# Sorting a mixture-of-experts kernel's experts by token count, and giving the 14 smallest 64 places and two products in place of three

## The chip, the cores and the metric

The kernel runs on one core of one Trainium2 chip. The time is the device time of one execution in microseconds (us). The engines are called as the profile calls them: PE (matrix products; PEld is its loading of the stationary operand), DVE (vector), ACT (scalar), POOL (general, here gathers and scatters), and SP (it issues the transfers of weights; its queue is SPq).

## The reference, cut to what matters

Two layers on 1024 tokens of width 1024. Each is a mixer (a gated convolution in layer 0, sliding-window attention in layer 1), a norm, a mixture of experts and a norm. The experts' part, with the bookkeeping left out:

```python
def hierarchical_moe(x, w_grp, w_exp, wg, wu, wd):
    ...
    g_idx = jnp.argmax(g_logits, axis=-1)          # one of 4 groups for each token
    ...
    top_p, top_i = lax.top_k(e_prob, TOP_K)        # 2 of the 8 experts of the group
    ...
    counts = jnp.zeros((N_EXPERTS,), jnp.int32).at[eid].add(1)
    ...
    def run_block(args):                           # a block: up to 128 tokens of one expert
        xb, e = args
        hid = jax.nn.silu(xb @ wg[e]) * (xb @ wu[e])
        return hid @ wd[e]
```

There are 32 experts in a layer. `wg[e]` and `wu[e]` are 1024 by 512, `wd[e]` is 512 by 1024, all float32: 6.29 MB an expert. 2048 pairs of token and expert are spread over the 32 experts as the tokens choose, so an expert has 64 on the mean, some have many more and some fewer.

## The kernel before

Every expert has a block of 128 places. An expert with more than 128 tokens gets further blocks after all the others (the overflow, `NOV`). A float32 product is made from parts: each operand is split into a high and a low part, and `mm3` (L203 to L206) makes three products, high by high, high by low, low by high. The rows of tokens are the stationary operand (128 by 128), the weights the moving one (128 by 512).

The weights come in chunks of 1 MB, six to an expert: two for gate, two for up, two for down. SP issues their transfers in the order of use, as soon as there is room in one of the rings of raw buffers (12 buffers in the first six rounds of a layer, then 6). A chunk is split by ACT, which writes the high part as a cast (L164), and by DVE, which writes the low part as a difference (L165). The parts have room for four chunks, so that the cast of chunk k waits until PE has done with chunk k-4. `split_until` issues the splits in the program's order, three chunks ahead of the products (`ahead = 3`).

`experts` (L718) is one written-out sequence, and each engine executes its own instructions in this order. For expert e, with c its first chunk, one pass of the loop at L818 issues: the products of gate with chunk c; y_out (L764, ACT scales the finished rows of expert e-2, and POOL adds them to memory, L713); the split of c+3; gate with c+1; the split of c+4; silu (L833, ACT); up with c+2; the split of c+5; the transposes of the next expert's rows (`xpose`, L735, PE) and the gather for expert e+3 (L703, POOL); up with c+3; the product of silu and up (L848, DVE); the split of c+6; the split of the next expert's rows (`xsplit`: `xh` on ACT, `xl` on DVE); the down products of expert e-1, with the splits of c+7 and c+8; and `hid_pose`, which transposes the hidden rows (L771, PE) and splits them (`hh` on ACT, `hl` on DVE). The next pass begins with the products of the next gate. So the down products of an expert stand one pass behind, and `hid_pose` stands last on PE before the next expert's first product.

Beside the first experts DVE, POOL and PE still work out the gates of the places (`gates` L600 on, `slot_gates` L630 to L641): POOL makes one-hot tables (`goh`, `ga`), and PE sums them into `pgate`.

Of the kernel before, what the change touches and what calls it, by code (L numbers as in the profile page):

```python
# [11 lines left out]
F32 = mybir.dt.float32  # L12
# [21 lines left out]

@with_exitstack
def moe_net_kernel(ctx, tc, a, dbg=None):
# [35 lines left out]
    def expert_chunks(l):  # L72
        seq = []
        for e in range(NE + 1):
            if e < NE:
                for w in ("w_gate", "w_up"):
                    for h in range(2):
                        seq.append(rows(a[w][l, e], h * 512, 512))
            if e > 0:
                for h in range(2):  # L80
                    seq.append(rows(a["w_down"][l, e - 1], h * 256, 256))
# [15 lines left out]
    # The raw chunks lie in rings of two: two rings always, except that heads of q take the second during  # L97
    # the attention, a third from the output projection to the experts' last, and four chunks in the room of
    # the mixer's output, from when it has been read to the experts' last.
    rings = []  # L100
    turn = itertools.cycle(("raw", "raw", "rawc", "rawc"))
    for l, c0 in enumerate((mark["wout"], mark["wo"])):
# [7 lines left out]
        while len(rings) < c0 + 4 + 6 * NE:  # L110
            rings += four() + ["rawb"] * 2
    raws, hs, ls = {}, {}, {}
# [4 lines left out]
    def pump(eng=nc.sync):  # L117
        while st["load"] < min(len(chunks), st["limit"]):
# [12 lines left out]
            src = chunks[i][0]  # L131
            if i == 1:
                # the first two chunks come in alternate quarters, that the work may start
# [12 lines left out]
    # 32 KB in two halves: the mixers' output, chunks, the norm's rows, heads of q  # L146
# [49 lines left out]
    def warm(n, ps, tag, bufs):  # L196
        # products for nothing where the tensor engine waits, that its clock stays up
# [12 lines left out]
    # -------------------------------------------------------------- constants  # L210
# [4 lines left out]
    diff = const.tile([P, P], F32, name="diff")  # L215
# [10 lines left out]
    iota(wt, [[-1, NE]], base=NE)  # L226
    rowm = const.tile([P, NB], F32, name="rowm")
# [37 lines left out]
    # ------------------------------------------------- bias rows of attention  # L265
# [3 lines left out]
    def bias_rows(w, ps):  # L269
# [11 lines left out]
        # row q lies q further right, so that a plain rectangle of it holds the relative positions  # L281
# [25 lines left out]
            # v, tokens on partitions  # L307
# [26 lines left out]
            # u, channels on partitions  # L334
# [1116 lines left out]
```

## Time and profile before

| | us |
|---|---|
| runs of the kernel before | 2083.45, 2084.56, 2085.84 |
| median | 2084.56 |
| span of the profiled execution | 2086.2 |
| PE busy in it | 1931.8 (93%) |
| DVE busy | 1580.8 (76%) |
| ACT busy | 1206.1 (58%) |
| POOL busy | 476.9 (23%) |

The profile gives the profiled execution no other time than its span. A busy PE means that products were under way; the granted clock (PEclk) is that of PE, as a share of full speed. Idle time of an engine counts only where another engine waits for what it does next.

### The profile page before, as it was taken

What the parts mean: (1) busy time and instruction counts of PE and PEld (TensorE: products, weight loads), DVE (VectorE), ACT (ScalarE), POOL (GpSimd) and SP (SyncE); (2) the same over time, 40 slices, a digit from 0 to 9 for tenths busy, and PEclk for the clock granted to TensorE, in tenths of its full rate; (3) what the DMA queues carried; (4) which work ended last, traced back from release to release, by engine and by line L of the source; (5) the groups of instructions that cost most, each with busy time, mean ns of one, the idle gap of its engine ahead of it and who ended that gap; (6) DMA issues with size and microseconds to landing.
All of it is one profiled execution on the core that took longest, in us unless ns stands there. A gap on an engine that the chain in (4) does not pass through costs nothing. (4 is left out here: it accounts for less than half of the span.)

```text
span 2086.2 us, 24852 instructions
## 1 busy us (share of the span) xinstructions
PE 1931.8 (93%) x9264; PEld 1565.7 (75%) x9264; DVE 1580.8 (76%) x2020; ACT 1206.1 (58%) x1246; POOL 476.9 (23%) x319
## 2 busy tenths in 40 slices
PE   8999998899999999998598989979999999999990
PEld 7888786687778888887487767757877888888870
DVE  3533587599888888887643996976898888888876
ACT  4211211477677777776454872125777777777763
POOL 0100003622111211212300552146121112112116
PEclk9999998899999999999799999989999999999995
DMA  6141536599969999997511006366999699999983
GB/s 249 41 122 41 192 112 242 192 335 371 345 228 363 371 364 377 369 371 281 225 41 62 21 21 232 125 248 219 374 357 355 218 379 360 368 376 364 380 282 145
DMA packets 97215, 527.59 MB, mean 253 GB/s; under 512 B 19668, under 2 KB 21732, under 8 KB 43840
## 3 DMA queue, kind: packets, MB, share of 16 engines
q1 hardware_dynamic: 76992, 487.41, 61.6%
q0 software_dynamic: 20096, 38.52, 7.4%
q8 instruction: 75, 1.23, 0.2%
q14 instruction: 52, 0.43, 0.1%
HBM read 501.58 MB, written 62.94 MB: 271 GB/s over the span
## 5 line engine op out<-in xcount | busy, mean ns | idle before, releaser
L165 DVE TENSOR_TENSOR l<-raw,h 128x2048 fp32r<-128x2048 f32 (+2 forms) x356 | 797.4, 2261 | 108.3 <-ACT h L164 104.0
L164 ACT CAST h<-raw 128x2048 fp32r<-128x2048 f32 (+1 forms) x363 | 678.2, 1884 | 130.9 <-PE pu L206 38.0
L713 POOL DMA_INDIRECT acc<-y,idx x64 | 127.5, 1993 | 605.7 <-ACT y L764 578.9
L204 PE MATMUL pu<-h,xh 128*128 128x512 f32 x512 | 209.5, 409 | 0.0
L204 PE MATMUL pg<-h,xh 128*128 128x512 f32 x512 | 208.6, 407 | 0.0
L204 PE MATMUL pd<-h,hh 128*128 128x512 f32 x512 | 203.2, 397 | 1.4 <-ACT hh L164 1.4
L206 PE MATMUL pg<-h,xl 128*128 128x512 f32 x512 | 203.0, 397 | 1.0 <-DVE xl L165 1.0
L206 PE MATMUL pu<-h,xl 128*128 128x512 f32 x512 | 203.1, 397 | 0.0
L205 PE MATMUL pu<-l,xh 128*128 128x512 f32 x512 | 202.9, 396 | 0.0
L206 PE MATMUL pd<-h,hl 128*128 128x512 f32 x512 | 202.0, 395 | 0.0
L205 PE MATMUL pg<-l,xh 128*128 128x512 f32 x512 | 201.7, 394 | 0.0
L205 PE MATMUL pd<-l,hh 128*128 128x512 f32 x512 | 201.4, 393 | 0.0
L703 POOL DMA_INDIRECT xg<-x1d,idx x64 | 96.6, 1510 | 354.0 <-PE pt L735 340.2
L164 ACT CAST xh<-pt 128x1024 fp32r<-128x1024 f32 x66 | 67.0, 1016 | 126.5 <-PE pu L205 110.2
L848 DVE TENSOR_TENSOR sg<-sg,pu 128x512 f32<-128x512 f32 x64 | 44.0, 687 | 110.8 <-PE pu L206 110.8
L206 PEld LDWEIGHTS pg<-h,xl 128*128 128x128 f32 x512 | 96.0, 188 | 25.2 <-DVE xl L165 1.9
L206 PEld LDWEIGHTS pd<-h,hl 128*128 128x128 f32 x512 | 96.0, 187 | 24.9 <-DVE hl L165 0.9
L206 PEld LDWEIGHTS pu<-h,xl 128*128 128x128 f32 x512 | 96.6, 189 | 23.7
L165 DVE TENSOR_TENSOR l<-ry,h 128x2048 fp32r<-128x2048 f32 x48 | 109.9, 2296 | 5.9 <-ACT h L164 5.9
L204 PEld LDWEIGHTS pd<-h,hh 128*128 128x128 f32 x512 | 96.0, 187 | 24.4 <-ACT hh L164 1.7
L205 PEld LDWEIGHTS pd<-l,hh 128*128 128x128 f32 x512 | 96.0, 187 | 23.1
L204 PEld LDWEIGHTS pu<-h,xh 128*128 128x128 f32 x512 | 97.6, 191 | 20.1
(326 smaller groups left out, 3844.8 us busy)
## 6 DMA issues: line engine op xcount, KB each, us to landing
raw<-in_w_gate SPq DMA_DIRECT2D x128, 1024.0 KB, 8.3
raw<-in_w_up SPq DMA_DIRECT2D x104, 1024.0 KB, 10.5
raw<-in_w_down SPq DMA_DIRECT2D x104, 1024.0 KB, 10.6
ry<-in_w_up SPq DMA_DIRECT2D x24, 1024.0 KB, 8.1
ry<-in_w_down SPq DMA_DIRECT2D x24, 1024.0 KB, 10.0
raw<-in_w_in SPq DMA_DIRECT2D x8, 1024.0 KB, 6.4
x1d<-xr SPq DMA_DIRECT2D x16, 512.0 KB, 2.7
acc<-xr SPq DMA_DIRECT2D x16, 512.0 KB, 3.9
```

Source lines behind the costliest of these rows:

```text
L164: (high or nc.scalar.copy)(h, x)
L165: (eng or nc.vector).tensor_tensor(l, x, h.bitcast(F32), op=OP.subtract)
L204: nc.tensor.matmul(out, sh, mh, start=start, stop=False)
L205: nc.tensor.matmul(out, sh, ml, start=False, stop=False)
L206: nc.tensor.matmul(out, sl, mh, start=False, stop=stop)
L703: nc.gpsimd.indirect_dma_start(out=rows, out_offset=None, in_=src, in_offset=bass.IndirectOffsetOnAxis(ap=idx, axis=0), bounds_check=T - 1 ...
L713: nc.gpsimd.indirect_dma_start(out=acc, out_offset=bass.IndirectOffsetOnAxis(ap=idx, axis=0), in_=rows, in_offset=None, bounds_check=T - 1 ...
L848: nc.vector.tensor_tensor(sg, sg, pu, op=OP.mult)
```

## The change

Each layer's experts are sorted on the chip by their token counts. Of the 32, the first three stay as they are (the experts 0 to 2, since their weights are loaded before the counts are known). The other 29 are put in order: 15 heavy ones, and the 14 smallest, the light ones, with 64 places each. The light ones are taken in pairs; a pair is one unit, with one gather, one set of transposes and one split for its 2 x 64 rows. The units go in the order heavy, heavy, heavy, then seven times (light pair, heavy, heavy), then a heavy one: 25 units, 32 experts.

For a light expert the high parts of its 64 rows and the low parts of the same 64 rows stand side by side as one stationary operand of 128 columns. Two products with a weight tile then make in the upper and the lower half of the result what three made, and one product that was not made before (low by low). The halves are added later: ACT copies the lower half out of `pg`, DVE adds it to the upper half, silu follows, and the same for `pu`. In the down products the hidden rows stand as [high, low, high], so that [high, low] and [low, high] serve as the two stationary operands in the three products of `mm3`; their number stays.

`sort` and `sort_gates` are new. They make ranks out of comparisons of the counts, a selection matrix from the ranks, and the order and the places by products with it. For every place from the fourth on, SP reads the expert's number from `order` and computes the address of each of the six chunks before it issues the transfer. Some scratch tiles are shared that were apart before.

```diff
+NS, NH, NL = 3, 15, 14
+CAP = 64
+UNITS = ["heavy"] * NS + ["light", "heavy", "heavy"] * (NL // 2)
+UNITS += ["heavy"] * (NS + NH + NL // 2 - len(UNITS))
...
+    def source(s):
...
+        l, p, w, r0, n = s
+        if p < NS:
+            return rows(a[w][l, p], r0, n)
+        if (l, p) not in experts_of:
+            col = PLACES[p][2]
+            experts_of[l, p] = nc.values_load(order_of[l][0:1, col:col + 1], engines=[mybir.EngineType.SP], min_val=0,
...
+        return a[w][l][bass.ds(experts_of[l, p], 1), r0:r0 + n].rearrange("o (p k) f -> p (o k) f", p=P)
...
+    def sort(w, ps, R):
...
+        nc.tensor.matmul(t[:, 0:NE], ones16, last, start=True, stop=True)
+        nc.tensor.matmul(t[e, 32:33], last, ones16[:, 0:1], start=True, stop=True)
...
+        nc.vector.scalar_tensor_tensor(key, R["cnt"][e], 64.0, orderr[e], op0=OP.mult, op1=OP.add)
+        nc.vector.scalar_tensor_tensor(own, t[e, 32:33], 64.0, orderc[e], op0=OP.mult, op1=OP.add)
+        nc.vector.tensor_scalar(more, key, own, None, op0=OP.is_gt)
+        nc.vector.tensor_reduce(place, more, axis=AX.X, op=OP.add)
...
+        nc.vector.tensor_scalar(sel[e], slots[e, 0:NE], place, None, op0=OP.is_equal)
...
+        yield
+        nc.tensor.matmul(t[0:1, 64:96], ecol[e], sel[e], start=True, stop=True)
+        nc.tensor.transpose(t[e, 128:256], ix[:, 0:NE], ident)
...
+        nc.tensor.matmul(t[:, 512:512 + NE], ixT[e], sel[e], start=True, stop=True)
...
+                    if lo is None:
+                        sh = h[:, 4 * half + k, j]
+                        nc.tensor.matmul(out, sh, hs[c][:, sl], start=first, stop=False)
+                        nc.tensor.matmul(out, sh, ls[c][:, sl], start=False, stop=last)
+                    else:
+                        mm3(out, h[:, 4 * half + k], lo[:, 4 * half + k], hs[c][:, sl], ls[c][:, sl], first, last)
...
+                    if light(p):
+
+                        nc.scalar.copy(sg[CAP:], pg[CAP:])
+                    else:
+                        nc.scalar.activation(sg, pg, AF.Silu)
...
+                    if light(p):
+                        nc.vector.tensor_tensor(sg[0:CAP], pg[0:CAP], sg[CAP:], op=OP.add)
...
-                    nc.vector.tensor_tensor(sg, sg, pu, op=OP.mult)
                     split_until(min(c + 3 + ahead, last - 1))
...
+                    if light(p):
+                        nc.scalar.activation(sg[0:CAP], sg[0:CAP], AF.Silu)
+                    else:
+                        nc.vector.tensor_tensor(sg, sg, pu, op=OP.mult)
...
+                    if p < NE - 1:
+                        split_until(c + ahead)
+                if light(p):
+                    nc.scalar.copy(sg[CAP:], pu[CAP:])
+                    nc.vector.tensor_tensor(pu[0:CAP], pu[0:CAP], sg[CAP:], op=OP.add)
+                    nc.vector.tensor_tensor(sg[0:CAP], sg[0:CAP], pu[0:CAP], op=OP.mult)
...
```

In layer 0, place 19 is the first expert of a light pair after the change. In the rows that follow, a number behind a tile's name is its chunk (133 to 135 are split with gate and the first half of up, 136 with the second half, 137 and 138 with the down products). DVE's order for this place before, from the first split of the pass to the last:

```order
682 L165 TENSOR_TENSOR l133_5588<-raw133_5447,h133_5587 128x2048
683 L165 TENSOR_TENSOR l134_5606<-raw134_5465,h134_5605 128x2048
684 L165 TENSOR_TENSOR l135_5626<-raw135_5485,h135_5625 128x2048
685 L848 TENSOR_TENSOR sg19_5611<-sg19_5611,pu19_5569 128x512
686 L165 TENSOR_TENSOR l136_5657<-raw136_5516,h136_5656 128x2048
687 L165 TENSOR_TENSOR xl20_5663<-pt20_5631,xh20_5662 128x1024
688 L165 TENSOR_TENSOR l137_5680<-raw137_5539,h137_5679 128x2048
689 L165 TENSOR_TENSOR l138_5698<-raw138_5557,h138_5697 128x2048
```

And after the change:

```order
720 L205 TENSOR_TENSOR l133_5497<-raw133_5359,h133_5496 128x2048
721 L205 TENSOR_TENSOR l134_5511<-raw134_5377,h134_5510 128x2048
722 L205 TENSOR_TENSOR l135_5527<-raw135_5397,h135_5526 128x2048
723 L1003 TENSOR_TENSOR sg19_5516<-pg19_5481,sg19_5516 64x512
724 L205 TENSOR_TENSOR l136_5542<-raw136_5427,h136_5541 128x2048
725 L205 TENSOR_TENSOR l137_5565<-raw137_5453,h137_5564 128x2048
726 L1039 TENSOR_TENSOR pu19_5482<-pu19_5482,sg19_5516 64x512
727 L1040 TENSOR_TENSOR sg19_5516<-sg19_5516,pu19_5482 64x512
728 L205 TENSOR_TENSOR l138_5586<-raw138_5471,h138_5585 128x2048
729 L925 TENSOR_TENSOR hid19_5596<-ph19_5591,hid19_5596 128x4x64
```

`sg19` by `pu19`, which stood behind three differences, is now the last of three small operations (L1003, L1039, L1040), and stands behind five differences. The split of the next rows (`xl20`) has gone from this place; it stands with the second expert of the pair.

ACT's order for the same place before:

```order
270 L164 CAST h133_5587<-raw133_5447 128x2048
271 L164 CAST h134_5605<-raw134_5465 128x2048
272 L833 ACTIVATE sg19_5611<-pg19_5568 128x512
273 L164 CAST h135_5625<-raw135_5485 128x2048
274 L164 CAST h136_5656<-raw136_5516 128x2048
275 L164 CAST xh20_5662<-pt20_5631 128x1024
276 L164 CAST h137_5679<-raw137_5539 128x2048
277 L164 CAST h138_5697<-raw138_5557 128x2048
```

And after the change:

```order
282 L204 CAST h133_5496<-raw133_5359 128x2048
283 L204 CAST h134_5510<-raw134_5377 128x2048
284 L996 COPY sg19_5516<-pg19_5481 64x512
285 L204 CAST h135_5526<-raw135_5397 128x2048
286 L204 CAST h136_5541<-raw136_5427 128x2048
287 L1018 ACTIVATE sg19_5516<-sg19_5516 64x512
288 L204 CAST h137_5564<-raw137_5453 128x2048
289 L1038 COPY sg19_5516<-pu19_5482 64x512
290 L204 CAST h138_5585<-raw138_5471 128x2048
291 L924 CAST hid19_5596<-ph19_5591 128x4x2x64
```

Silu (L833 before, L1018 after) has moved from behind two casts to behind four, and waits there for DVE's addition (L1003). Two copies from the accumulators (L996, L1038) are new, and the second stands behind the fifth cast.

## Rows read from the trace of the kernel before

**Rows 1.** The page's head.

```profile
span 2086.2 us, 24852 instructions
```

**Rows 2.** Stretch of one expert: length; busy PE, PEld, DVE, ACT, POOL; PEclk; DMA share, GB/s.

```profile
687.20:705.40 18.20, 18.20 (x86) 14.91 (x85) 15.77 (x10) 14.22 (x10) 3.59 (x2) 1.00 1.00 363
```

**Rows 3.** Waits of the DMA-issuing engine, 1890 to 1985: total, times, longest.

```profile
SPq L139 <- DVE l L165: 83.2, 31, 4.3
```

**Rows 4.** Timeline of DVE: start, duration, line, operation, tiles, count; in brackets idle before.

```profile
703.94 4.48 DVE L165 TENSOR_TENSOR l<-raw,h 128x2048 fp32r<-128x2048 f32 x2
...
709.49 6.90 DVE L165 TENSOR_TENSOR l<-raw,h 128x2048 fp32r<-128x2048 f32 x3 [0.47 <-ACT h L164]
718.21 0.69 DVE L848 TENSOR_TENSOR sg<-sg,pu 128x512 f32<-128x512 f32 x1 [1.82 <-PE pu L206]
...
721.02 1.22 DVE L165 TENSOR_TENSOR xl<-pt,xh 128x1024 fp32r<-128x1024 f32 x1
```

**Rows 5.** Timeline of PE in the same stretch.

```profile
705.40 0.63 PE L771 MATMUL ph<-ident,sg 128*128 128x128 f32 x4
705.78 0.48 PE L204 MATMUL pg<-h,xh 128*128 128x512 f32 x1
706.10 0.40 PE L205 MATMUL pg<-l,xh 128*128 128x512 f32 x1
...
707.27 0.39 PE L204 MATMUL pg<-h,xh 128*128 128x512 f32 x1
...
714.26 1.11 PE L735 MATMUL pt<-ident,xg 128*128 128x128 f32 x8
715.13 0.48 PE L204 MATMUL pu<-h,xh 128*128 128x512 f32 x1
```

**Rows 6.** Timeline of ACT in the same stretch.

```profile
706.06 0.59 ACT L164 CAST hh<-ph 128x512 fp32r<-128x512 f32 x1 [1.36 <-PE ph L771]
...
707.55 3.71 ACT L164 CAST h<-raw 128x2048 fp32r<-128x2048 f32 x2
711.67 0.60 ACT L833 ACTIVATE sg<-pg 128x512 f32<-128x512 f32 x1 [0.41 <-PE pg L206]
...
717.98 1.01 ACT L164 CAST xh<-pt 128x1024 fp32r<-128x1024 f32 x1 [1.61 <-PE pu L205]
```

**Rows 7.** Stretches with gaps of PE, and those behind them; columns of group 2.

```profile
404.00:406.60 2.60, 0.02 (x1) 0.00 (x0) 2.37 (x2) 1.82 (x1) 2.60 (x3) 1.00 0.99 413
406.60:413.40 6.80, 5.62 (x21) 4.88 (x22) 0.19 (x1) 0.00 (x0) 4.07 (x9) 0.50 0.70 271
519.10:521.00 1.90, 0.04 (x1) 0.05 (x1) 1.90 (x5) 1.90 (x2) 0.00 (x0) 1.00 1.04 379
522.60:526.10 3.50, 3.50 (x13) 2.87 (x12) 3.50 (x7) 0.60 (x1) 0.00 (x0) 0.51 1.04 332
1033.10:1036.10 3.00, 0.00 (x0) 0.00 (x0) 3.00 (x2) 0.58 (x1) 0.81 (x1) 1.00 0.05 21
1036.10:1040.00 3.90, 3.89 (x17) 3.25 (x18) 3.56 (x3) 0.00 (x0) 0.00 (x0) 1.00 0.70 248
```

**Rows 8.** Timeline of DVE where layer 0 starts its experts.

```profile
372.03 0.19 DVE L604 TENSOR_TENSOR ge<-lg,mx 128x32 f32<-128x32 f32 x1
```

**Rows 9.** Timeline of POOL in the same place.

```profile
382.78 0.37 POOL L637 TENSOR_SCALAR ga<-A,gate 128x32 f32<-128x32 f32 x1 [2.33 <-DVE gate L623]
```

**Rows 10.** Waits of PE where layer 0 starts its experts, 365 to 425.

```profile
PE pgate L630 <- POOL ga L637: 3.8, 5, 2.6
```

**Rows 11.** Waits of ACT, 1890 to 1985: total, times, longest.

```profile
ACT h L164 <- DMA raw<-in_w_gate: 7.0, 7, 1.8
```

**Rows 12.** Stretches with few transfers, and one with many; columns of group 2.

```profile
600.00:617.00 17.00, 16.43 (x79) 13.32 (x78) 15.24 (x18) 11.53 (x10) 1.55 (x2) 1.00 0.17 40
1620.00:1640.00 20.00, 19.43 (x94) 15.82 (x93) 17.78 (x19) 14.25 (x10) 3.06 (x2) 1.00 0.34 108
1003.00:1009.00 6.00, 3.22 (x14) 2.85 (x15) 5.32 (x6) 5.58 (x12) 2.31 (x3) 0.50 1.03 421
```

More of the change, by code (lines that the diff above doesn't have):

```diff
@@ L32, with places @@
 EARLY = (1, 6)
+NS, NH, NL = 3, 15, 14
+CAP = 64
+UNITS = ["heavy"] * NS + ["light", "heavy", "heavy"] * (NL // 2)
+UNITS += ["heavy"] * (NS + NH + NL // 2 - len(UNITS))
+def places():
+    out, heavy, light = [], 0, NH
+    for u, kind in enumerate(UNITS):
+        if u < NS:
+            out.append((u, 0, NH + NL + u))
+        elif kind == "heavy":
+            out.append((u, 0, heavy))
+            heavy += 1
+        else:
+            out += [(u, 0, light), (u, 1, light + 1)]
+            light += 2
+    return out
+PLACES = places()
 @with_exitstack
@@ new lines, in gather @@
+            def gather(u):
+                if u < NS:
+                    idx = R["idx"][:, u:u + 1]
+                elif u == U:
+                    idx = R["ovidx"][:, 0:1]
+                else:
+                    col = next(q[2] for q in PLACES if q[0] == u)
+                    idx = R["sidx"][:, col:col + 1]
+                    if UNITS[u] == "light":
+                        idx = R["twos"][:, (col - NH) // 2:(col - NH) // 2 + 1]
+                gather_rows(xg[(u + U) % 2], x1d, idx)
@@ new lines, in light, with gu @@
+            def light(p):
+                return p < NE and UNITS[PLACES[p][0]] == "light"
+            def gu(p, half, c, out):
+                u, j = PLACES[p][:2] if p < NE else (U, 0)
+                h, lo = xT[u]
+                for k in range(4):
+                    first, last = half == 0 and k == 0, half == 1 and k == 3
+                    sl = slice(k * 512, (k + 1) * 512)
+                    if lo is None:
+                        sh = h[:, 4 * half + k, j]
+                        nc.tensor.matmul(out, sh, hs[c][:, sl], start=first, stop=False)
+                        nc.tensor.matmul(out, sh, ls[c][:, sl], start=False, stop=last)
+                    else:
+                        mm3(out, h[:, 4 * half + k], lo[:, 4 * half + k], hs[c][:, sl], ls[c][:, sl], first, last)
@@ L753, in down @@
+            def down(p, half, c):
                 if half == 0:
-                    pd[e] = ps.tile([P, D], F32, name=f"pd{e}", tag="pd" if e < NE - 1 else "pt", bufs=1)
-                h, lo = hT[e]
+                    pd[p] = ps.tile([P, D], F32, name=f"pd{p}", tag="pd" if p < NE - 1 else "pt", bufs=1)
+                h, lo = hT[p]
                 for k in range(2):
@@ L777, in extra @@
+                hT[p] = (h, lo)
             def extra(e):
@@ L802, in experts @@
             ov = {}
-            why = "it follows from the counts"
             gather(0)
@@ L840, in experts @@
+                    gu(p, 0, c + 2, pu)
+                    next(sorting, None)
+                    split_until(min(c + 2 + ahead, last))
+                    if light(p):
+                        nc.vector.tensor_tensor(sg[0:CAP], pg[0:CAP], sg[CAP:], op=OP.add)
+                    extra(p)
+                    if ends and u + 1 < U:
+                        xpose(u + 1)
+                        if p == 0:
                             xsplit(1)
-                    if e + 3 < NE:
-                        gather(e + 3)
@@ L852, in experts @@
+                    if 0 < p < NE - 1 and ends:
+                        xsplit(u + 1)
                     c += 4
-                if e == NE:
-                    y_out(e - 2)
+                if p == NE:
+                    y_out(p - 2)
                     xe = nc.values_load(R["meta"][0:1, 1:2], engines=[mybir.EngineType.SP], min_val=0,
@@ L929, in overflow_blocks @@
             ps = pool(f"ops{l}", space=PSUM, st=s)
-            why = "it follows from the counts"
             s.enter_context(tc.If(nblk > 1))
```

237 lines of the change are left out of this document (156 added, 81 removed).

## The prediction

> **What bounds the kernel now.** I read the page's head first, then the stretches of single experts, then the timelines of PE, DVE and ACT over one of them, and last the places where PE stood still. The head gives a span of 2086.2 us [rows 1], with PE busy for 93% of it by the table above. In the middle of layer 0 one expert takes 18.20 us, and in it PE is busy for 18.20 us, DVE for 15.77 and ACT for 14.22; the 16 transfer engines have a share of 1.00 at 363 GB/s [rows 2]. So two things are full at once, PE and the transfers, and DVE follows with 87%. The share of the transfers is no proof that they limit, since SP issues one only when a raw buffer is free: late in layer 1 it stands for 83.2 us of 95 at waits for DVE's differences, which free the buffers [rows 3]. Within an expert the limit is PE, and DVE waits for it: the product of silu and up (L848) had idled 1.82 us for up [rows 4]. The reader is to see there also that DVE's other wait, 0.47 us before the first difference of a pass, is for ACT.
>
> **What is taken from PE.** Five products take 707.27 - 706.10 = 1.17 us, 0.234 each [rows 5]. A heavy expert has 48 of gate and up and 24 of down: 72 x 0.234 = 16.8 us, with 0.87 us of transposes of rows (714.26 to 715.13) and 0.38 of hidden rows (705.40 to 705.78), 18.1 us. A light expert saves 16 products, 3.74 us. For 14 in each of two layers that is 28 x 3.74 = 105 us of PE's time, about 5% of the run. Half of the pairs' transposes goes too (14 x 0.87 = 12 us). The question is whether what stands beside PE can follow.
>
> **The chain of a light expert.** I walk the new order with durations of before; t = 0 is the expert's first gate product, 705.78 in the trace.
>
> - The first difference of a pass begins at 709.49, t = 3.71 [rows 4]. What it waits for is ACT's queue: the cast of the hidden rows (706.06), y_out, and the first weight cast (707.55) [rows 6]. All three remain in the same order, and the hidden rows' cast starts from the transposes, which are the last work of the previous expert on PE. So this delay stays.
> - Three differences take 6.90 us [rows 4]: t = 10.6. ACT keeps ahead: its first two casts end at 711.26 (t = 5.5), the new copy is priced as silu, 0.60 us [rows 6], and the third cast (1.86, half of 3.71) ends by t = 8.1.
> - DVE adds the half of `pg`. This operation is not in the trace; it has the width of the product at L848, 512 elements for each partition, so 0.69 us [rows 4] is my price; half would be a lower bound, since half of the partitions is used, and a whole difference (2.24) the upper. t = 11.3.
> - Silu can only start now on ACT: t = 12.0. Behind it stands the cast of c+7, to 13.9. DVE meanwhile takes the fourth difference, to 13.6, waits 0.4 us for that cast, and takes the fifth, t = 14.0 to 16.3.
> - Only then come the addition for `pu` and the product with silu, 2 x 0.69: t = 17.7. The copy they need ran on ACT from 13.9 to 14.5.
> - The transposes of hidden rows wait for it, t = 17.75 to 18.1. That is the next expert's t = 0.
>
> PE's own work ends early: 32 products of gate and up and 24 of down take 13.1 us; it waits 0.4 us for the first difference (t = 6.0, when its 24 products are done at 5.6) and 0.4 for the second (8.3, when up is done at 7.9), and is through at t = 14.0. Then it stands still for 3.7 us. So the first expert of a pair takes 18.1 us, as a heavy one does.
>
> The second has the split of the next unit's rows as well: ACT 1.01 us [rows 6], DVE 1.22 less an overlap of 0.1 [rows 4]. Its product comes at t = 18.7, the period is 19.1, the gap 4.7. A pair takes 37.2 us for 36.4 before. With the pitch that operations have back to back (4.48 for two differences, 3.71 for two casts) it is 36.2. I take +0.4 a pair, for 14 pairs **+6 us**, with bounds of -3 and +11. The freed time of PE becomes idle time, since before, L848 stood behind three differences and waited for PE; now PE waits for it behind five.
>
> **The clock.** PE now stands still twice in a pair, for 3.7 and 4.7 us. The trace has three gaps of the kind [rows 7]. After 2.60 us of standing (404.0 to 406.6) the granted clock was 0.50, its lower level of 1.2 GHz, for 6.80 us; after 1.90 (519.1 to 521.0) it was 0.51 over 522.6 to 526.1, 3.5 us; after 3.00 (1033.1 to 1036.1) it stayed at 1.00. So gaps of this length mostly cost the clock, not always. At half clock H us of PE do the work of H/2. Where a heavy expert follows, PE is the bound and loses H/2: 1.75 us (H = 3.5) or 3.4 (H = 6.8). Where the second light follows, its gap covers it but for waits at the two half-chunks, 0.1 to 1.6 us. That makes 1.85 to 5.0 a pair. I take 2.9, nearer to the shorter fall, and that four gaps in five bring it: 2.3 x 14 = **+32 us**. Bounds: 0, and 14 x 5 = 70.
>
> **Start of each layer.** `sort` puts nine or so small DVE operations and nine products of PE ahead of the gates. A small operation of DVE takes 0.19 us here [rows 8], so they are 2 us; the products are taken as 0.234 each, 2 us. POOL's first gate table waited 2.33 us for DVE's gates [rows 9], and PE's longest wait there, 2.6 us, the gap before 406.6, is for these tables [rows 7, 10]: what delays DVE here delays PE. A result of PE reaches ACT in 0.28 us (705.78 to 706.06) [rows 5, 6], and the sort goes to and fro some six times, 1.7 us. Rounded down for what lies beside other work I take 5 us a layer, **+10 us**. Lower bound 2 (all beside PE's first experts), upper 20 (the tables' wait of 2.6 comes for each step of the sort too).
>
> **SP's reading of the order.** Its loads of registers and address arithmetic are not in the trace of before. SP waits 83.2 us of 95, for some five experts, about 16 us each [rows 3]: that is the cover, and I cost it at nothing. They count only if an expert's take longer than those 16 us, or if a chunk's landing is late already. The gathers go from 32 to 25 a layer, on POOL, which is busy for 3.59 us of 18.20 [rows 2]: nothing.
>
> **End of layer 1.** There ACT waited 7.0 us in seven waits for gate weights to land [rows 11]; slower pairs give the transfers time. **-2 us**, bounds -5 and 0.
>
> **The sum.** 6 + 32 + 10 - 2 = +46. It is made against the profiled span of 2086.2, which lies 1.6 above the median of the runs, with no other time shown for that execution; from the median 2084.6 + 46 = **2131 us**. The changes and their sizes are small beside the span, so I carry the sum over as it is.
>
> **Rivals.**
>
> *The light chain is shorter than walked (faster).* The chain is one loop: hidden transposes, ACT's three operations, five differences, product. If it runs below about 17.4 us (the additions at 0.35 because of 64 partitions, no wait for the cast of c+7, waits before the first difference shorter because PE is done early), a pair takes 35 us or less, and the gaps shrink. Then the transfers decide. They stood idle for 0.83 x 17 = 14 us at the ring's change in layer 0 and 0.66 x 20 = 13 in layer 1 [rows 12]. If 363 GB/s is what they can do, only these 27 us are to be had, less the 10 of the start: 2068. But over 1003 to 1009 they moved 421 GB/s [rows 12], 6.29 MB in 14.9 us; then pairs of 34 us would give 14 x 2.4 = 34 on top of 27 less 10, and about 2035. Against it: two of the three terms of the loop, ACT's head and the differences, are rows as they stand.
>
> The Trainium skill, "DMA: Bandwidth & Descriptors", section "Where 436 GB/s comes from", says that for transfers between memory and SBUF the memory's share of a core, about 358 GB/s, binds. By that an expert's 6.29 MB would need 17.6 us, and 64 experts could gain at most 38 us by any relief of PE, my estimate from that page. This trace disagrees: 363 is passed by the 421 of [rows 12]. So I do not use that limit.
>
> *The clock stays up (a small loss).* One gap of 3.00 us did not lower it [rows 7]. If none does, 6 + 10 - 2 = 14 remains: 2099, with the bounds of the rest 2079 to 2115.
>
> *Each gap costs the long fall (a larger loss).* With 6.8 us at half clock after each, 14 x 5.0 = 70 in place of 32: 2169; with the upper bounds of the rest, 2184.
>
> **How the numbers follow.** The forecast has a chance of 0.50 and is the likeliest, the long fall 0.12, the clock that stays 0.18, the faster chain 0.18, and 0.02 is left for cases that I have not named. Two executions of this kernel differ by about 0.1%, so 0.2% (4 us) is what can be told from no change. Faster: 0.18 and a little of the second rival, 0.20. Same: 0.06, from the second rival near its lower bound. Slower: 0.74. The forecast's own range is 2105 to 2160. The range for 8 in 10 reaches down past the lower end of the clock's rival and into the faster one, 2078, and up to 2180; the deeper gains (0.15) and the last 0.04 are left out.
>
> **What would show it.** Right: in light experts PE idles 3 to 5 us before the hidden transposes, released by DVE's product with silu, and DVE no longer waits for PE's up there; a pair of light experts takes 37 to 40 us; granted clock of 0.5 after such gaps, in the stage where it was 1.00; a transfer share below 1; PE's busy products fewer by 28 x 16. Wrong: light experts of 16 us or less; a first difference well before t = 3.7; gaps below 2 us. SP released last by its own register loads, or ACT waiting for weights that have not landed in the middle of a layer, would show that the part that I cost at nothing is not.

## The result and the profile after

| | us |
|---|---|
| runs after the change | 2119.71, 2122.60, 2123.80, 2125.53 |
| median | 2123.2 |
| median before, same chip | 2085.2 |
| ratio of the two | 1.0173, 95% interval 1.0161 to 1.0186 |
| span of the profiled execution | 2122.2 |

The medians lie 38 us apart, and the ratio makes it 36 us, 34 to 39 by its interval: slower. The page of the changed kernel, with its span, the busy times, the granted clock and the share of the transfers in 40 slices:

```profile
span 2122.2 us, 24672 instructions
...
PE 1862.6 (88%) x8728; PEld 1501.3 (71%) x8728; DVE 1613.4 (76%) x2108; ACT 1224.2 (58%) x1288; POOL 445.9 (21%) x307
...
PEclk9999998899999899899799999988999999999995
DMA  6131436599969999997511006365999699999974
```

PE is busy for 69 us less than before and the span is 36 us longer [rows 1]. PE's instructions, products and transposes, went from 9264 to 8728: 28 x 16 products and 14 x 8 transposes fewer, and a few more for the sort. Three digits of the clock's row in the expert stages went from 9 to 8 (places 14, 17 and 28).

Next two groups of light, light, heavy, heavy in layer 0, a stretch from one expert's hidden transposes to the next's; columns as in [rows 2]:

```profile
680.40:698.30 17.90, 14.05 (x62) 10.69 (x60) 16.14 (x11) 14.42 (x11) 1.59 (x1) 0.97 1.02 381
698.30:718.30 20.00, 17.07 (x69) 13.70 (x69) 17.09 (x12) 15.43 (x12) 4.35 (x2) 0.84 1.01 384
718.30:739.10 20.80, 20.80 (x84) 17.02 (x85) 15.65 (x10) 14.26 (x10) 3.15 (x2) 0.85 0.93 332
739.10:757.10 18.00, 18.00 (x86) 14.99 (x86) 15.96 (x10) 14.18 (x10) 3.15 (x2) 1.00 0.96 349
757.10:775.00 17.90, 14.07 (x62) 10.70 (x60) 16.15 (x11) 14.42 (x11) 1.58 (x1) 1.00 1.00 372
775.00:794.10 19.10, 16.23 (x68) 13.04 (x68) 17.02 (x12) 15.42 (x12) 4.34 (x2) 0.91 1.00 366
794.10:812.30 18.20, 18.16 (x84) 15.16 (x85) 15.62 (x10) 14.18 (x10) 3.22 (x2) 1.00 0.97 360
812.30:830.20 17.90, 17.90 (x85) 14.95 (x84) 15.86 (x10) 14.18 (x10) 3.15 (x2) 1.00 1.00 377
```

The first expert of a pair takes 17.9 us, not less than a heavy one, and PE is busy for 14.1 of it. The second takes 19.1 or 20.0, the heavy behind it 18.2 or 20.8, and a heavy one with nothing before it 18.0, where it was 18.2 [rows 2]. So the first group takes 76.7 us and the second 73.1, for 72.9 before. The columns of the clock tell the two apart. The gaps of the first group, and what follows each:

```profile
694.50:698.30 3.80, 0.13 (x2) 0.06 (x1) 3.73 (x4) 2.36 (x2) 0.00 (x0) 0.85 1.01 425
698.30:704.00 5.70, 5.70 (x16) 4.52 (x17) 3.92 (x3) 4.99 (x4) 1.57 (x1) 0.50 1.02 427
715.30:718.30 3.00, 0.07 (x2) 0.06 (x1) 2.94 (x4) 1.59 (x1) 0.00 (x0) 0.89 1.05 425
718.30:724.50 6.20, 6.20 (x17) 4.92 (x18) 4.43 (x3) 3.44 (x4) 1.46 (x1) 0.50 0.98 359
```

After 3.8 us of standing the clock is 0.50 for 5.7 us, and after the second gap of 3.0 us for 6.2. The two gaps of the second group, with what follows the first of them:

```profile
771.30:774.90 3.60, 0.00 (x0) 0.00 (x0) 3.54 (x4) 2.26 (x2) 0.00 (x0) 1.00 1.00 419
774.90:779.10 4.20, 4.13 (x13) 3.32 (x14) 2.47 (x3) 3.44 (x4) 1.56 (x1) 0.59 1.02 419
791.30:794.10 2.80, 0.00 (x0) 0.00 (x0) 2.73 (x4) 1.47 (x1) 0.00 (x0) 1.00 1.01 419
```

The first gap was followed by a fall again (0.59 over 4.2 us). The second left the clock at 1.00, as the stretch from 794.10 above shows, and the heavy expert behind it took 18.2 us. By the idle time that the trace gives ahead of the hidden transposes, the second gaps of the two groups are equally long: 2.93 and 2.92 us.

The DVE timeline in the first light expert, whose first gate product stands at about 680.8:

```profile
684.48 6.70 DVE L205 TENSOR_TENSOR l<-raw,h 128x2048 fp32r<-128x2048 f32 x3 [1.46 <-ACT h L204]
691.21 0.68 DVE L1003 TENSOR_TENSOR sg<-pg,sg 64x512 f32<-64x512 f32 x1
691.92 2.29 DVE L205 TENSOR_TENSOR l<-raw,h 128x2048 fp32r<-128x2048 f32 x1
694.39 2.29 DVE L205 TENSOR_TENSOR l<-raw,h 128x2048 fp32r<-128x2048 f32 x1 [0.17 <-ACT h L204]
696.72 0.69 DVE L1039 TENSOR_TENSOR pu<-pu,sg 64x512 f32<-64x512 f32 x1
697.44 0.68 DVE L1040 TENSOR_TENSOR sg<-sg,pu 64x512 f32<-64x512 f32 x1
```

The first difference begins at t = 3.7, the addition for gate ends at 11.1, the fifth difference runs from 13.6 to 15.9, and the product with silu (L1040) ends at 17.3. It is the order shown in the section on the change, with no idle time but 0.17 us. PE in the same place:

```profile
694.20 0.40 PE L246 MATMUL pd<-h,hid 128*128 128x512 f32 x1
698.27 0.71 PE L918 MATMUL ph<-ident,sg 64*128 64x64 f32 x4 [3.67 <-DVE sg L1040]
698.91 0.79 PE L886 MATMUL pg<-h,xx 128*128 128x512 f32 x1
```

The last down product starts at 694.20 and the hidden transposes 3.67 us of idle time later, released by `sg` L1040. Over the whole run the view of the tile `ph` gives for this wait, in us and times:

```profile
  DVE sg L1040: 76.6, 27
```

### The profile page after: what moved, and what is told of

It is laid out like the page before. It is cut to its first block, busy times and chain, and to the rows that moved or that the text cites. A ratio compares the mean times of both kernels' runs of the same rounds, so it can differ in the third digit from the quotient of the medians.

```text
span 2122.2 us, 24672 instructions
## 1 busy us (share of the span) xinstructions
PE 1862.6 (88%) x8728; PEld 1501.3 (71%) x8728; DVE 1613.4 (76%) x2108; ACT 1224.2 (58%) x1288; POOL 445.9 (21%) x307
## 5 line engine op out<-in xcount | busy, mean ns | idle before, releaser
L824 POOL DMA_INDIRECT acc<-y,sidx x64 | 101.4, 1585 | 721.9 <-ACT y L910 708.6
L245 PE MATMUL pd<-l,hid 128*128 128x512 f32 x512 | 201.3, 393 | 1.3 <-DVE l L205 0.6
L244 PE MATMUL pd<-h,hid 128*128 128x512 f32 x512 | 201.1, 393 | 1.4 <-ACT hid L204 1.4
L246 PE MATMUL pd<-h,hid 128*128 128x512 f32 x512 | 201.4, 393 | 0.0
L205 DVE TENSOR_TENSOR l<-ry,h 128x2048 fp32r<-128x2048 f32 x48 | 109.4, 2286 | 18.1 <-ACT h L204 18.1
L244 PE MATMUL pg<-h,xx 128*128 128x512 f32 x272 | 116.1, 427 | 0.0
L245 PEld LDWEIGHTS pd<-l,hid 128*128 128x128 f32 x512 | 96.2, 188 | 26.5 <-DVE l L205 5.6
L244 PEld LDWEIGHTS pd<-h,hid 128*128 128x128 f32 x512 | 96.4, 188 | 22.4 <-ACT hid L204 1.7
L246 PEld LDWEIGHTS pd<-h,hid 128*128 128x128 f32 x512 | 96.2, 188 | 21.6 <-DVE hid L205 0.9
L245 PE MATMUL pg<-l,xx 128*128 128x512 f32 x272 | 111.3, 409 | 0.0
L246 PE MATMUL pg<-h,xx 128*128 128x512 f32 x272 | 111.2, 409 | 0.0
L244 PE MATMUL pu<-h,xx 128*128 128x512 f32 x272 | 110.8, 407 | 0.0
L246 PE MATMUL pu<-h,xx 128*128 128x512 f32 x272 | 107.3, 395 | 0.0
L245 PE MATMUL pu<-l,xx 128*128 128x512 f32 x272 | 107.0, 393 | 0.0
L244 PE MATMUL pm<-h,yx 128*128 128x512 f32 x256 | 103.9, 406 | 2.1 <-ACT yx L204 1.2
L886 PE MATMUL pg<-h,xx 128*128 128x512 f32 x224 | 102.3, 457 | 0.0
L245 PE MATMUL pm<-l,yx 128*128 128x512 f32 x256 | 100.4, 392 | 1.2 <-DVE l L205 1.2
```

Source lines behind the costliest of these rows:

```text
L205: (eng or nc.vector).tensor_tensor(l, x, h.bitcast(F32), op=OP.subtract)
L244: nc.tensor.matmul(out, sh, mh, start=start, stop=False)
L245: nc.tensor.matmul(out, sh, ml, start=False, stop=False)
L246: nc.tensor.matmul(out, sl, mh, start=False, stop=stop)
L824: nc.gpsimd.indirect_dma_start(out=acc, out_offset=bass.IndirectOffsetOnAxis(ap=idx, axis=0), in_=rows, in_offset=None, bounds_check=T - 1 ...
L886: nc.tensor.matmul(out, sh, hs[c][:, sl], start=first, stop=False)
```

## The experiments

The kernel before was run again beside the experiments, on the same chip. Its medians were 2088.8 us (all heavy; operations moved ahead; 15 and 12 products for nothing; gates ahead of the sort), 2086.6 (17 and 19 products; both edits together; the first pad in the kernel before), 2087.1 (the other pads) and 2088.4 (one more operation; weights without the order). Ratios are to these.

### All experts heavy, but sorted

```diff
-UNITS = ["heavy"] * NS + ["light", "heavy", "heavy"] * (NL // 2)
-UNITS += ["heavy"] * (NS + NH + NL // 2 - len(UNITS))
+UNITS = ["heavy"] * (NS + NH + NL)
```

> All 32 experts are taken as heavy ones, 3 products each, in the sorted order; the sort, the reading of the order by SP and the computed addresses stay. My theory: in the trace after the change the first hidden transposes come 7 us later than before in layer 0, and layer 1 begins its experts another 9 us later, both from the sort; the rest of the loss lies in the light pairs. So 2085 + 16 = 2101 us (2096 to 2106), experts at 18.2 us with no gaps of the matmul engine. Rival one: reading the order costs in every expert; then periods above 18.2 us and 2110 or more. Rival two: the sort costs nothing and all is in the light pairs: 2085.

Measured: 2093.1 us, ratio 1.0024 (1.0014 to 1.0034): +5 us, not +16, a miss. The light pairs are most of the loss. But the start was as late as with them: layer 1's first hidden transposes come 24.2 us behind its first gate product, 24.3 in the changed kernel, 16.6 before. What paid for it was in the stretch of one expert:

```profile
728.70:746.60 17.90, 17.90 (x85) 14.95 (x84) 15.03 (x9) 13.50 (x11) 3.78 (x2) 1.00 1.02 369
```

17.9 us for 18.2, with the same products. And after 800 us the transfers came late (ACT's waits from 800 to 965, total, times, longest):

```profile
ACT h L203 <- DMA raw<-in_w_gate: 27.3, 18, 2.2
```

So some 15 us for the sort were right at their place, and something that I had not counted gave time back in each heavy expert; the pad runs below are about that. But little of it stayed. From the first hidden transposes to the last, the experts of the two layers took 580.1 and 578.4 us, for 581.5 and 580.1 before: 3 us less in all, since from 800 us on (and late in layer 1) weights landed late. SP waited there for free buffers for 131.7 of 165 us, and 359 GB/s were moved for 374 before, so that the late weights are not shown to come from a limit of the transfers' rate. Another 5.5 us lie between the layers (from layer 0's last hidden transposes to layer 1's first gate product, 423.3 us for 428.9), in work that is the same; that stretch differs from trace to trace without any edit there.

### A light expert's small operations moved ahead

```diff
                     gu(p, 1, c + 1, pg)
+                    if light(p):
+                        nc.scalar.copy(sg[CAP:], pg[CAP:])
+                        nc.vector.tensor_tensor(sg[0:CAP], pg[0:CAP], sg[CAP:], op=OP.add)
                     split_until(min(c + 1 + ahead, last))
...
                     gu(p, 1, c + 3, pu)
+                    if light(p):
+                        nc.scalar.copy(sg[CAP:], pu[CAP:])
+                        nc.vector.tensor_tensor(pu[0:CAP], pu[0:CAP], sg[CAP:], op=OP.add)
+                        nc.vector.tensor_tensor(sg[0:CAP], sg[0:CAP], pu[0:CAP], op=OP.mult)
                     split_until(min(c + 3 + ahead, last - 1))
```

(Silu goes behind the split of c+4; the same operations are taken out at their old places.)

> The changed kernel with the small operations of a light expert moved ahead: the copy and the addition for gate straight behind gate's last product, ahead of the split of the next chunk, and the copy, addition and product for up straight behind up's last product, ahead of the splits of two chunks. No work is added or left out. My theory: the order on DVE's and ACT's queues makes the matmul engine idle. With the product behind three differences and not five it is ready at about t = 12.8, when the down products still run to 14.5; then DVE's own work bounds, about 16.5 us for a light expert. The 22 us lost in the expert stages go, and 14 pairs gain some 3 us each: 2123 - 22 - 42 = 2060 us (2045 to 2085), gaps below 1 us. Rival one: transfers bind at the 363 GB/s of the middle of a layer; then four experts take 69.3 us and the time is 2065 to 2075, with the waits for weights that have not landed as the sign of it. Rival two: the additions themselves, not their place, hold the light experts: no better than 2115.

Measured: 2057.4 us, ratio 0.9848 (0.983 to 0.9865). DVE in a light expert, first gate product at about 672.4:

```profile
676.18 2.29 DVE L205 TENSOR_TENSOR l<-raw,h 128x2048 fp32r<-128x2048 f32 x1 [1.44 <-ACT h L204]
678.50 0.68 DVE L994 TENSOR_TENSOR sg<-pg,sg 64x512 f32<-64x512 f32 x1
679.22 2.29 DVE L205 TENSOR_TENSOR l<-raw,h 128x2048 fp32r<-128x2048 f32 x1
681.67 2.29 DVE L205 TENSOR_TENSOR l<-raw,h 128x2048 fp32r<-128x2048 f32 x1 [0.17 <-ACT h L204]
684.00 0.69 DVE L1019 TENSOR_TENSOR pu<-pu,sg 64x512 f32<-64x512 f32 x1
684.72 0.68 DVE L1020 TENSOR_TENSOR sg<-sg,pu 64x512 f32<-64x512 f32 x1
685.33 6.68 DVE L205 TENSOR_TENSOR l<-raw,h 128x2048 fp32r<-128x2048 f32 x3
```

The product with silu ends at 685.4, t = 13.0, before PE is done with the down products (the last starts at 686.71 and the hidden transposes at 687.04, with no gap); the three differences left stand behind it. A first light expert now takes 15.0 us, a second 16.1 to 18. One group of four, and the middle of the layer:

```profile
672.10:739.90 67.80, 65.65 (x297) 52.41 (x296) 64.18 (x40) 58.21 (x43) 33.19 (x7) 1.00 1.02 394
640.00:965.00 325.00, 313.50 (x1415) 250.91 (x1413) 302.38 (x183) 271.64 (x201) 83.27 (x32) 1.00 0.98 379
```

67.8 us for four experts with the clock at 1.00; over 325 us DVE is busy for 302 (93%) and PE for 313 (96%), and the transfers move 379 GB/s, 394 in the quick group. ACT waits for weights in the same stretch:

```profile
ACT h L204 <- DMA raw<-in_w_gate: 11.8, 12, 1.9
```

So the loss was the place of six small operations, three on DVE and three on ACT: with the same work the kernel is 66 us faster than the changed one and 31 faster than the one before. The clock's part of the loss is in the 66, since the gaps are gone. What bounds now was not taken apart. A heavy expert with nothing ahead of it still takes 17.94 us, all of it busy PE; the one behind a pair takes 18.9. PE's waits in this stretch are for DVE's differences, ACT's in part for weights that land late.

### Products for nothing in the gaps

```diff
                 pt = ps.tile([P, 4, P], F32, name=f"ph{p}", tag="ph", bufs=1)
+                if light(p):
+                    for _ in range(15 if PLACES[p][1] == 0 else 12):
+                        nc.tensor.matmul(pt, ones16, ones16[:, None, :].to_broadcast([P, 4, P]), start=True, stop=True)
```

> The changed kernel with products for nothing in the gap before a light expert's hidden transposes, 15 for the first of a pair and 12 for the second, some 0.21 us each. My theory: the gaps cost twice, and the larger part is the clock that falls in them; the chain of DVE and ACT is as long as before and stays the limit, so that work added to the matmul engine costs nothing. In the groups of light, light, heavy, heavy where the clock stayed up, four experts took 73.2 us for 72.9 before, elsewhere 76.8; all at 73.2 gives about 2104 us (2099 to 2110). Rival one: the clock is not what costs, the chain alone is: 2123. Rival two: the matmul engine still is the limit in light experts, and 27 us of products on it in 14 pairs make it slower: 2130 or more.

Measured: 2128.0 us, ratio 1.0198 (1.0172 to 1.0224): a miss, by the number nearer to the second rival. The first light expert of a pair still took 17.8 us with 15 products more, so PE was not the limit there. But the second gap was not filled: its 12 products took 2.8 us. What was left, and what followed, is shown by two stretches:

```profile
721.80:723.40 1.60, 0.02 (x1) 0.03 (x1) 1.53 (x4) 0.29 (x1) 0.00 (x0) 1.00 0.99 415
723.50:727.30 3.80, 3.80 (x12) 3.02 (x13) 2.36 (x2) 3.19 (x3) 1.33 (x1) 0.61 1.01 405
```

1.6 us of standing were left, and the clock fell there in 8 of 10 pairs (not in every one, as the next expectation says). In two pairs of each layer (experts 7, 8, 11 and 12), where the gap was 1.7 us or less, the 27 products made the pairs longer.

> Again the changed kernel with products for nothing in the gaps, now 17 for the first and 19 for the second of a pair, and none for the two pairs of each layer's first rounds, where 27 products had to go into gaps of 1.3 to 1.7 us and made the pairs longer by 2 to 3 us. With 12 in the second gap 1.6 us of it were left, and the clock fell there in every pair for some 3.5 us. My theory: filled gaps keep the clock up, a group of four experts takes 72.8 us for 75 on the mean, ten groups: 2123 - 22 = 2101 us (2095 to 2108). Rival: the clock does not cost the end of the group, or falls none the less: 2120 or more.

Measured: 2103.0 us, ratio 1.0076 (1.0048 to 1.0104), as expected. A group of four:

```profile
679.20:752.10 72.90, 72.67 (x334) 56.15 (x333) 64.69 (x40) 58.20 (x43) 11.47 (x7) 1.00 1.00 374
```

72.9 us with the clock at 1.00 throughout, and the first light expert still 17.8 us, the second 18.9. So the clock's part of the loss is 2123 - 2103 = 20 us in the ten pairs that were filled, and more work on PE was the way to see it. The other four pairs kept their falls (0.83 to 0.92 over an expert), which are not in the 20.

### One more operation in the chain

```diff
+                    nc.vector.tensor_tensor(pg[0:CAP], pu[0:CAP], sg[CAP:], op=OP.add)
                     nc.vector.tensor_tensor(pu[0:CAP], pu[0:CAP], sg[CAP:], op=OP.add)
```

> The changed kernel with one more DVE operation in each light expert, the addition for up done a second time, into a place that nobody reads, 0.69 us. My theory: a light expert is a chain through DVE from its first difference to the product with silu, so the operation makes each of the 28 light experts longer by its whole duration: 28 x 0.69 = 19 us, 2123 + 19 = 2142 us (2137 to 2152, the longer gaps may cost some more of the clock). Rival: the chain has slack, because ACT or the weights come later anyway; then 2123 to 2130.

Measured: 2148.7 us, ratio 1.0293 (1.027 to 1.0316): 25 us more than the changed kernel. The first light expert of a pair takes 18.49 us for 17.89, the wait ahead of its transposes is 4.27 for 3.67:

```profile
702.73 0.71 PE L918 MATMUL ph<-ident,sg 64*128 64x64 f32 x4 [4.27 <-DVE sg L1041]
```

The 6 us above 19 agree with clocks that fell in more pairs (in this trace behind all eight second gaps of 3.5 to 3.7 us, in the changed kernel's behind four of the eight of 2.9), but that part was not separated. There is no slack in the chain.

### The gates ahead of the sort

```diff
-                    next(sorting, None)
                     split_until(min(c + ahead, last))
                     extra(p)
+                    next(sorting, None)
```

> The changed kernel with the first step of the sort put behind the gates' small DVE operations instead of ahead of them, at the first expert of each layer. My theory: the sort delays the gates on DVE by 3.7 us, POOL's tables wait for them and the matmul engine for the tables, so each layer starts 4 us later from this alone: 2123 - 8 = 2115 us (2111 to 2119). Rival: the start is late for the sort's own chain between the matmul engine and DVE, or for the gather that waits for the sorted places, and the order of the two does not matter: 2121 to 2125.

> The two edits together: a light expert's small operations ahead of the splits, and the gates ahead of the first step of the sort. My theory: they act in different places and add up. Against the kernel of before the first gives 31 us; the second took 5 us off the way from layer 1's first gate product to its first hidden transposes, 4 off the whole run. 2057 - 4 = 2053 us (2047 to 2057). Rival: with light experts of 15 to 16.5 us the transfers set the end of each layer, and an earlier start only lengthens waits for weights: 2057 or more.

Measured: 2119.2 us alone, ratio 1.0142 (1.0112 to 1.0172), against 1.0173 (1.0161 to 1.0186) of the changed kernel: 4 us less, but the intervals overlap. With the operations moved ahead, 2057.5, 0.9849 (0.9816 to 0.9882), no gain over 2057.4: the rival's number. Waits from 365 to 432 in the changed kernel, then with the gates first:

```profile
POOL ga L744 <- DVE order L709: 6.8, 1, 6.8
...
PE pgate L737 <- POOL ga L744: 5.9, 5, 2.5
```

```profile
PE pgate L737 <- POOL ga L744: 3.5, 5, 2.5
```

What stands ahead of the gates in the changed kernel's DVE queue is less the small operations (1.6 us) than a wait for PE, whose product of the counts comes behind the first gate products:

```profile
382.87 0.19 DVE L695 COPY cnt<-sort 128x32 f32<-128x32 f32 x1 [2.70 <-PE sort L690]
```

The way from layer 1's first gate product to its first hidden transposes went from 24.3 to 19.2 us, in both kernels. So 5 us of the 7.7 lost there came from the order of the two; some of it is given back at the next expert (25.1 and 26.5 us to its transposes, 24.3 in the changed kernel). The two edits together gained nothing over the first alone: from the second hidden transposes of a layer on, their expert stages agree within 1 us, but layer 1's first gate product came 4.3 us later after layer 0's last hidden transposes. The edit does not touch that work. This stretch took 423.3 to 431.7 us in the other traces and 434.4 here, so most of the 4.3 us are its scatter from trace to trace; the rest stays open.

### Weights loaded without the order

```diff
-        if p < NS:
-            return rows(a[w][l, p], r0, n)
...
+        return rows(a[w][l, p], r0, n)
```

> The changed kernel without the reading of the order and without computed addresses: the weights of expert p are loaded for place p, as in the kernel before, while rows and gates stay those of the sorted experts (so the products are of other weights than the reference's). My theory: SP's reading is hidden behind its waits for raw buffers, and nothing changes: 2123 us (2119 to 2127). Rival: reading and addresses hold up the transfers in each expert, or at the first sorted one; then at least 10 us less, 2113 or below.

Measured: 2125.7 us, ratio 1.0181 (1.0157 to 1.0204), the same as with the order. SP's waits in the changed kernel, 640 to 965:

```profile
SPq L179 <- DVE l L205: 234.9, 95, 4.8
SPq L179 <- DVE hid L925: 30.8, 9, 3.4
```

266 of 325 us are waits for free buffers. Reading the order costs nothing that can be told.

### The places of operands

The same instructions took 17.94 us an expert in the sorted kernels and 18.22 before. In the changed kernel the scratch tiles moved, and with them the addresses: the experts' stationary operands lie at a multiple of 128 bytes in their partition, before 32 beyond one; the split weights 64 beyond, before 0 (first pair of buffers) and 96 (second). This is how the programs lay out their tiles; no trace shows addresses.

```diff
+            nc.gpsimd.memset(w.tile([P, 8], F32, name=f"pad{l}", tag="pad", bufs=1), 0.0)
             xT, hT, pd, pgs = {}, {}, {}, {}
```

> The changed kernel with 32 bytes ahead of the experts' tiles, so that their stationary operands lie 32 beyond a multiple of 128 as in the kernel before; the split weights stay where the changed kernel has them. The computation is the same. My theory: heavy experts go back from 17.94 to 18.22 us, light ones are bound by the chain of DVE and ACT and stay: 36 x 0.28 = 10 us more than 2123, 2133 us (2129 to 2138). That would be what the change costs without the luck of its places. Rival: the place of the stationary operand counts only together with that of the weights: 2121 to 2127.

Measured: 2134.0 us, ratio 1.0223 (1.0197 to 1.0249), as expected. A heavy expert, columns as above:

```profile
737.70:755.90 18.20, 18.20 (x86) 14.93 (x85) 15.95 (x10) 14.23 (x10) 3.10 (x2) 1.00 0.97 348
```

18.2 us again, with the first light of a pair at 17.88, as without the pad. The pad moves all tiles behind it in the experts' pool; of those PE reads only stationary operands. The 11 us are not this alone: in this trace the clock fell behind 7 of the 8 second gaps of about 2.8 us, for 4 of 8 in the changed kernel's. The same pad with 24 elements for 8 in the kernel before (and `diff` put into `y0` to make room):

> The kernel before, with nothing computed otherwise, but 96 bytes ahead of the experts' tiles, so that the stationary operands lie at addresses that are multiples of 128 bytes and no longer 32 beyond one (room for it comes from one scratch table put where the changed kernel has it). Heavy experts take 17.94 us in every sorted kernel and 18.22 in the kernel before, with the same instructions: a product every 0.229 us for 0.233. My theory: the place of the stationary operand in its partition does it, as the sorted kernels have it at multiples of 128. Then 64 x 0.28 = 18 us: 2085 - 18 = 2067 us (2063 to 2072). Rival: the place of the moving operands, 96 beyond a multiple of 128 here as before and 64 in the sorted kernels, or something else: 2083 to 2088.

Measured: 2081.4 us, ratio 0.9975 (0.9962 to 0.9989): 5 us of the 18, outside both ranges. Experts took 18.00 and 18.18 us in turn, about half of the gain on the mean:

```profile
705.69:723.69 18.00, 18.00 (x86) 14.97 (x85) 15.67 (x10) 14.25 (x10) 3.57 (x2) 1.00 1.01 389
723.69:741.87 18.18, 18.18 (x86) 14.97 (x84) 15.94 (x10) 14.22 (x10) 3.73 (x2) 1.00 0.98 372
```

With 16 elements there, and 8 ahead of the second pair of buffers:

> The kernel before with 64 bytes ahead of the experts' tiles and 32 ahead of the second pair of buffers of split weights, so that the stationary operands and all split weights lie at multiples of 128 bytes; the computation is the same. With the stationary operands alone at such places, experts took 18.18 and 18.00 us in turn, those with four chunks in the second pair of buffers (96 beyond a multiple) and those with two. My theory: each operand's place counts, a chunk in the second pair costs 0.09 us more, so all experts take 17.82 us: 64 x 0.40 = 26 us less than 2086, 2060, or a few us above it where weights come late as they did at 17.94: 2063 us (2058 to 2072). Rival: the turns have another cause, as the number of loads from each ring, and the second pad does nothing: 2078 to 2083.

Measured: 2078.2 us, ratio 0.9959 (0.9945 to 0.9973), the rival's number: the experts still take 17.93 and 18.12 in turn.

```profile
703.03:720.96 17.93, 17.93 (x85) 14.96 (x84) 15.65 (x10) 13.49 (x11) 3.60 (x2) 1.00 1.02 389
720.96:739.09 18.13, 18.13 (x86) 14.98 (x85) 15.96 (x10) 15.06 (x11) 3.70 (x2) 1.00 0.96 373
```

The turns have another cause, which stays open. And the operations moved ahead, with all these operands at multiples of 128:

> The changed kernel with the light experts' small operations ahead of the splits, and with split weights and stationary operands at multiples of 128 bytes (the weights lie 64 beyond one in the changed kernel). The computation is the same. My theory: 36 heavy experts of 17.82 us for 17.94 give 4 us, light ones are bound by DVE and by the transfers: 2057 - 4 = 2053 us (2048 to 2058). Rival: DVE at 93% and the transfers bind the heavy ones behind a pair as well, since they catch up there: 2057.

Measured: 2057.4 us, ratio 0.9855 (0.9838 to 0.9871): no gain in time, though heavy experts went from 17.94 to 17.86. By the traces the experts' two stages were shorter by 2.8 us (558.4 and 559.8 for 559.8 and 561.2), and the rest of that execution was 1.5 us longer. So it is not shown that DVE and the transfers bind the heavy experts there.

## Why the prediction was right, step by step

The forecast was 2131 us, the time 2123.2; the sign and the mechanism held. That the number came so near is in part luck: the clock was put 12 us too high and 10 us of the places were left out, against 11 us too little for the chain and the starts. By its terms (measured against 2085.2):

- **The chain.** The walk gave 18.1 and 19.1 us for the two experts of a pair, with gaps of 3.7 and 4.7; the trace has 17.9 and 19.1, 3.67 and 2.9. The second gap is smaller since PE, slowed by the first, is done later: with the first filled, the second was 12 products and 1.6 us long. Each station of the walk lies within 0.4 us of the timeline. Against 18.22 an expert a pair is longer by 17.89 + 19.17 - 36.44 = 0.6 us, and the heavy one behind it by 0.2 against other heavy ones: 14 x 0.8 = 12 us for the +6. This counts all pairs alike, and some 0.3 of the 0.8 is the clock's, since with both gaps filled a pair and the heavy one behind it took 54.9 us for 55.2. That the chain decides is shown from both sides: an operation more costs 25 us, the same operations moved ahead give 66.
- **The clock.** The step was right in kind, its size was off: 20 us by the filled gaps, for +32. Every gap of 3.7 us lowered the clock, but what follows it is the second light expert, which has slack for most of it (19.2 us behind a fall of 3.4 us, 20.0 to 20.3 behind one of 6.8). Only the second gap hits a heavy one, and its fall came in 6 of the 14 pairs, not in four of five: in the two with 3.5 us, in four of the eight with 2.9, and in none of the four with 1.3 to 1.5.
- **The start of the layers.** 7.7 us a layer from the first gate product to the first hidden transposes, 15 for the +10. The reason given, DVE's gates late and POOL's tables behind them, is shown for 5 of the 7.7, of which the next expert takes some 1 to 2 back. What the term missed is DVE's wait of 2.70 us for PE's product of the counts. Its other parts are less well founded: only two of the sort's products stand ahead of the gates, and the 0.28 us from PE to ACT run from the start of the next product, while the row's own end (705.40 + 0.63) lies 0.03 us before ACT's start.
- **SP's reading of the order, the gathers.** Nothing for the reading, as costed; the gathers were not tested apart.
- **The end of layer 1.** The -2 had no ground: experts took 18.22 us there before as in the middle of a layer, so ACT's waits for weights cost nothing that could be saved. No such wait is left in the trace after.
- **Left out.** The places of the operands: -10 us for 36 heavy experts, by the pad that undoes it. The trace of before gave no sign of it. The sum of what was measured is 12 + 20 + 15 - 10 = 37, for 38 between the medians; without the luck of the places the changed kernel took 2134. The two traces, stage by stage, give the same: 7.9 and 7.7 us at the starts, 12.3 and 9.8 in the experts behind them (12 + 20 - 10 = 22), 1.3 between the layers, -0.7 ahead of the first expert and -2.3 behind the last, 36 in all.

One slip in the rivals: by its terms the upper bound of the long fall is 2084.6 + 11 + 70 + 20 = 2186, not 2184.

The rival of a shorter chain was right about what would happen if the chain were shorter. Its bound with transfers at 363 GB/s was 2068; 379 to 394 GB/s were moved and 2057 came out. So the trace spoke rightly against about 358 GB/s as a limit, the figure of the Trainium skill, "DMA: Bandwidth & Descriptors", section "Where 436 GB/s comes from". Waits for weights did begin, though, where all experts took 17.9 us (27.3 us of them from 800 to 965 with all heavy but sorted), at 359 GB/s and with SP still waiting for buffers; what sets them stays open.

## What to carry to other kernels

Where one engine is full and the next is at 87%, work taken from the first is only worth what the queues of the others let through: write down, in queue order, what stands ahead of the one operation that the full engine will now wait for. Small operations added to an in-order queue belong ahead of the long ones that nobody waits for yet. And a gap of PE can cost twice, by its length and by the clock behind it; to price the second, fill the gap with work for nothing.

## What the runs showed of the hardware

- A product of 128 by 512 started every 0.233 us in the kernel before and every 0.229 in the changed one, over an expert 18.22 and 17.94 us. A pad of 32 bytes ahead of the stationary operands brought the 18.22 back. In the kernel before, the opposite shift gave 18.00 and 18.18 in turn, so that the stationary operand's place is not all of it.
- Second gaps of equal length, 2.93 and 2.92 us of idle PE, fell on either side: one was followed by 6.2 us at half clock, one by none. All gaps of 3.5 us and more were followed by a fall, and so were 8 of 10 gaps of 1.6 us that stood behind 12 products for nothing.
- The transfers' share was 1.00 at 363 GB/s before and 1.02 at 394 over 68 us after: the share did not tell how much was left. With experts at 17.9 us and less, waits for weights appear at 359 GB/s too.
